# Gate/up, down and per-layer gate products by Strassen's scheme on two problems of 544 tokens

## The chip, the cores and the metric

The kernel runs on one core of one Trainium2 chip. The time is the device time of one execution in microseconds, the median of several runs. The engines have their usual names: PE is TensorE (PEld its weight loads), DVE is VectorE, ACT is ScalarE, POOL is GpSimd, and SP is SyncE, which issues nearly all transfers here.

## The reference

One decoder layer works on 1024 prompt tokens and 64 sample tokens (8 sequences of 8), 1088 rows of 1024 features in all, everything in float32.

```
h  = rmsnorm(x, norm_mix);  q, k, v, ... ga, gb = split(h @ w_in)
o  = select_attend(...);    conv = short_conv(cg * xc, ...)
x += (sigmoid(ga) * o + sigmoid(gb) * (bg * conv)) @ w_out          # 1024 x 1024
h  = rmsnorm(x, norm_ffn);  g, u = split(h @ w_gate_up)             # 1024 x 5632
x += (silu(g) * u) @ w_down                                         # 2816 x 1024
gate = sigmoid(rmsnorm(x, norm_ple) @ w_ple_gate)                   # 1024 x 1024
x += (p @ w_ple) * gate
y  = rmsnorm(x, norm_final)
```

The change concerns the last four matrix products with the 1088 rows: out, gate/up, down and per-layer gate. This part is called the second half here.

## The kernel before

Activations lie transposed in SBUF, features on partitions and the 1088 tokens along the free axis, and each product keeps a weight block of 128 x 128 stationary and moves tokens past it. The tokens go in three chunks, `CH` = 384, 384 and 320. To keep float32 accuracy, every operand is split into a leading part rounded to the fast format (`hi`) and the remainder (`lo`), and each block takes three matmuls: hi·hi, hi·lo and lo·hi. A weight part of at most 512 columns a partition is fetched by SP into `wraw`; ACT writes `wh` from it and POOL subtracts to get `wl`. Two `wraw` and four pairs of `wh`/`wl` are in rotation (class `Weights`).

`run_group` goes chunk by chunk through a block: 24 matmuls into one PSUM bank (tag `pj`, three banks) for a contraction of 1024, and then one evacuation. For gate the evacuation is a Silu on ACT, for up a multiplication on DVE (`silu<-pj,silu`) followed by the split into `m_hi` (ACT) and `m_lo` (POOL). For out and down it is one addition on DVE into the residual `x1` (`x<-pj,x`). Gate/up and down alternate in three groups of 8, 7 and 7 blocks of 128 hidden features, so that `m` stays in SBUF.

Before gate/up and before the per-layer gate stands a norm. Per token chunk, ACT squares (`sq`), DVE adds the squares, PE sums over partitions (`po<-ones,sq`), DVE finds the reciprocal root in some 10 tiny instructions (`ns`), makes a diagonal (`dg`), PE spreads it (`at<-dg,ones`), and DVE, ACT and POOL make `hx`, `h_hi` and `h_lo` for 8 feature blocks. The first and last two blocks of a product are run as pairs per chunk, so that another chunk's products stand in PE's queue while one chunk's norm is worked out.

All engines execute in order. What order they get is decided while the program is built, by the class `Weaver`: it keeps a rough clock of each engine, runs the main stream of products, and lets side streams (norms, softmax, stores) put their instructions in when their inputs should be there. All arithmetic goes through its small helpers, so in the profile line L152 is a projection matmul, L148 another matmul, L159 a transpose, L102 a DVE tensor-tensor operation, L106 a DVE operation with a scalar and two tensors, L111 a DVE scalar operation, L117 a POOL tensor-tensor operation, and L98 an ACT operation.

Of the kernel before, what the change touches and what calls it, by code (L numbers as in the profile page):

```python
# [43 lines left out]


# [5 lines left out]
def tok_tiles(c):  # L51
    c0, n = CH[c]
    return [(c0 // P + j, min(P, T - c0 - j * P)) for j in range(-(-n // P))]

# [17 lines left out]
class Weaver:  # L72
    """Orders the instructions of several streams for the in-order engines."""
# [14 lines left out]
    # instructions, with a rough clock of each engine  # L88
# [29 lines left out]

    def recip(self, out, in_, n):
# [41 lines left out]
    # buffers: the ring of a tag holds the times at which its free ones came free  # L161
# [11 lines left out]
    # streams  # L173
# [104 lines left out]
def hybrid_decoder_step(ctx, tc, I, O):  # L278
# [18 lines left out]
    c2_scr = dram([KT, P, T], F32, "c2_scr")  # L297
    ple_scr = dram([KT, P, T], F32, "ple_scr")
# [4 lines left out]
    pp = ctx.enter_context(tc.tile_pool(name="ps", bufs=1, space=PSUM))  # L303
    PSB = {"pj": 3, "at": 2, "pt": 2, "po": 1}
    for t, n in PSB.items():
        W.add_tag(t, n)

    def psum(tag):
        W.cur.t = max(W.cur.t, W.take(tag))
        return pp.tile([P, 512], F32, tag=tag, name=tag, bufs=PSB[tag])  # L310

# [22 lines left out]
    def new_h(name):  # L334
        H["hi"] = apool.tile([P, KT, T], F32R, tag="A_hi", name=name + "_hi")
        H["lo"] = apool.tile([P, KT, T], F32R, tag="A_lo", name=name + "_lo")
# [15 lines left out]
    def sqrt_table():  # L352
        """Has the table of Sqrt loaded before it is waited for."""
# [5 lines left out]
    # ------------------------------------------------------------------  # L359
    # products with the activations: weight blocks stationary, token chunks moving  # L360
    class Weights:
        """Parts of at most 512 columns a partition: loaded, then split into a leading and a remaining part."""
        NP, NR = 4, 2

        def __init__(self):
            self.parts, self.nl, self.nv = [], 0, 0

        def add(self, src, shape):
            p = dict(src=src, shape=list(shape), done=False)
            self.parts.append(p)  # L370
            return p

        def load(self):
            if self.nl < len(self.parts):
                p = self.parts[self.nl]
                p["raw"] = wpool.tile(p["shape"], F32, tag="wraw", name="wraw", bufs=self.NR)
                p["t"] = W.dma(p["raw"], p["src"])
                self.nl += 1

        def pump(self, must=False, most=9):  # L380
            while most and self.nv < len(self.parts) and (self.nv < self.NP or self.parts[self.nv - self.NP]["done"]):
                p = self.parts[self.nv]
                if not must and p.get("t", 0.0) > W.T["pe"]:
                    break
                must, most = False, most - 1
                if self.nl <= self.nv:
                    W._flush(1e9)
                    while self.nl <= self.nv:
                        self.load()
                old, W.cur = W.cur, Stream(None)  # L390
                W.cur.t = max(W.T["pe"], p["t"])
                p["hi"] = wpool.tile(p["shape"], F32R, tag="wh", name="wh", bufs=self.NP)
                p["lo"] = wpool.tile(p["shape"], F32R, tag="wl", name="wl", bufs=self.NP)
                r = p.pop("raw")
                m = p["shape"][1] * p["shape"][2]
                W.act(p["hi"], r, AF.Copy, m)
# [1560 lines left out]
```

## Time and profile before

| what | value |
|---|---|
| runs | 2037.45, 2044.50 and 2044.59 us, median 2044.5 us |
| profiled execution | span 2039.7 us; it has no time of its own on record beside the span, and the span lies 4.8 us below the median of the runs |
| PE, matmuls | busy 1991.4 us, 98% |
| DVE | busy 918.3 us, 45% |
| ACT | busy 636.1 us, 31% |
| POOL | busy 701.4 us, 34% |
| transfers | 167.88 MB, mean 82 GB/s |

The shares are averages. In the first 1020 us (input projection, attention, convolution) DVE is busy in seven to nine tenths of many slices; in the second half it is busy in none to two tenths for long stretches, while PE shows nine tenths throughout.

### The profile page before, as it was taken

How to read it: one execution, taken by the hardware profiler on the slowest of the kernel's cores; microseconds unless marked ns; L12 is line 12 of the kernel's file. 1: busy time of each engine (PE TensorE's matmuls, PEld its weight loads, DVE VectorE, ACT ScalarE, POOL GpSimd, SP SyncE). 2: the span in 40 equal slices, each digit the busy share in tenths (PEclk: the TensorE clock that was granted, in tenths of full speed). 3: DMA queues.
4: the chain of work that ended last, by engine and by line, in shares of the span. 5: the costliest groups of instructions: out<-in, count | busy, mean ns of one | idle time of the engine just before them, and what ended most of it. 6: DMA issues, size and time to landing. Idle time of an engine off the chain costs nothing.

```text
span 2039.7 us, 31786 instructions
## 1 busy us (share of the span) xinstructions
PE 1991.4 (98%) x12065; PEld 1910.0 (94%) x12065; DVE 918.3 (45%) x2154; ACT 636.1 (31%) x1315; POOL 701.4 (34%) x672
## 2 busy tenths in 40 slices
PE   8999999999999999999999999999999999999998
PEld 5987788999999999779999899999999999999898
DVE  6636999899898885214224400011000110002734
ACT  5355433213433235333422322111222112222333
POOL 2533454223222233114423433322333223332483
PEclk9999999999999999999999999999999999999999
DMA  4664334222222122545541111111111111111133
GB/s 148 189 183 122 95 111 119 64 60 78 66 66 69 51 70 72 141 115 163 191 150 37 42 42 47 47 42 47 47 42 44 41 51 42 47 43 46 43 99 117
DMA packets 252980, 167.88 MB, mean 82 GB/s; under 512 B 26048, under 2 KB 247800, under 8 KB 252826
## 3 DMA queue, kind: packets, MB, share of 16 engines
q1 hardware_dynamic: 252582, 165.74, 27.6%
q8 instruction: 95, 1.56, 0.3%
q14 instruction: 59, 0.48, 0.1%
q10 hardware_dynamic: 244, 0.09, 0.0%
HBM read 126.59 MB, written 39.06 MB: 81 GB/s over the span
## 4 chain that ended last, share of the span: by engine, by line
PE 85%; DVE 5%; issue 1%; ACT 1%; POOL 1%; DMA 0%; SPq 0%; POOLq 0%; DVEq 0%; ACTq 0%
PE pj L152 74%; PE at L148 5%; PE po L148 4%; PE pt L159 3%; DVE hx L106 0%; DVE scores L106 0%; DVE ru L102 0%; DVE h_lo L102 0%; ACT h_hi L98 0%; DVE junk L1050 0%; DVE ns L1618 0%; DVE ns L1620 0%; DVE sq L102 0%; POOL wl L117 0%; POOL psmp L1377 0%
## 5 line engine op out<-in xcount | busy, mean ns | idle before, releaser
L152 PE MATMUL pj<-h_hi,wh 128*128 128x384 f32 (+2 forms) x2616 | 872.1, 333 | 0.3 <-ACT wh L98 0.3
L152 PE MATMUL pj<-h_lo,wh 128*128 128x384 f32 (+2 forms) x2616 | 857.8, 328 | 1.2 <-POOL h_lo L117 1.0
L152 PE MATMUL pj<-h_hi,wl 128*128 128x384 f32 (+2 forms) x2616 | 858.0, 328 | 0.7 <-POOL wl L117 0.7
L117 POOL TENSOR_TENSOR wl<-wraw,wh 128x512 fp32r<-128x512 f32 (+2 forms) x286 | 367.2, 1286 | 760.5 <-ACT wh L98 739.6
L152 PEld LDWEIGHTS pj<-h_hi,wh 128*128 128x128 f32 (+1 forms) x2616 | 493.0, 188 | 16.7 <-issue 12.5
L152 PEld LDWEIGHTS pj<-h_lo,wh 128*128 128x128 f32 (+1 forms) x2616 | 493.3, 189 | 5.6 <-POOL h_lo L117 2.1
L152 PEld LDWEIGHTS pj<-h_hi,wl 128*128 128x128 f32 (+1 forms) x2616 | 492.6, 188 | 1.7 <-POOL wl L117 1.1
L98 ACT ACTIVATE wh<-wraw 128x512 fp32r<-128x512 f32 (+2 forms) x286 | 177.1, 620 | 334.4 <-PE pj L152 310.9
L102 DVE TENSOR_TENSOR silu<-pj,silu 128x384 f32<-128x384 f32 (+1 forms) x66 | 35.3, 536 | 470.4 <-PE pj L152 466.1
L152 PE MATMUL pj<-m_hi,wh 128*128 128x384 f32 (+1 forms) x720 | 235.6, 327 | 0.0
L152 PE MATMUL pj<-m_hi,wl 128*128 128x384 f32 (+1 forms) x720 | 235.1, 327 | 0.0
L152 PE MATMUL pj<-m_lo,wh 128*128 128x384 f32 (+1 forms) x720 | 234.9, 326 | 0.0
L102 DVE TENSOR_TENSOR x<-pj,x 128x384 f32<-128x384 f32 (+1 forms) x96 | 51.4, 535 | 241.8 <-PE pj L152 237.7
L152 PEld LDWEIGHTS pj<-m_hi,wh 128*128 128x128 f32 x720 | 135.2, 188 | 0.3
L152 PEld LDWEIGHTS pj<-m_lo,wh 128*128 128x128 f32 x720 | 135.2, 188 | 0.3
L152 PEld LDWEIGHTS pj<-m_hi,wl 128*128 128x128 f32 x720 | 135.2, 188 | 0.0
L117 POOL TENSOR_TENSOR m_lo<-silu,m_hi 128x384 fp32r<-128x384 f32 (+1 forms) x66 | 64.1, 972 | 157.4 <-ACT m_hi L98 157.4
L1050 DVE TENSOR_SCALAR_CACHE_REDUCE junk<-scores,canda 128x384 uint8<-128x384 f32 (+3 forms) x132 | 107.3, 813 | 4.7
L117 POOL TENSOR_TENSOR rt<-rt,ru 128x384 fp32r<-128x384 f32 (+5 forms) x81 | 81.1, 1008 | 74.5 <-ACT ru L98 33.9
L98 ACT ACTIVATE m_hi<-silu 128x384 fp32r<-128x384 f32 (+1 forms) x66 | 33.5, 507 | 201.8 <-DVE silu L102 201.8
L1131 POOL TENSOR_SCALAR p<-p,mx 128x128 f32<-128x128 f32 (+7 forms) x64 | 50.5, 794 | 100.3 <-DVE mx L121 81.2
L1050 DVE TENSOR_SCALAR_CACHE_REDUCE junk<-scores,candb 128x896 uint8<-128x896 f32 x66 | 80.0, 1213 | 2.3
(244 smaller groups left out, 2149.3 us busy)
## 6 DMA issues: line engine op xcount, KB each, us to landing
wraw<-in_w_in SPq DMA_DIRECT2D x112, 256.0 KB
wraw<-in_w_gate_up SPq DMA_DIRECT2D x88, 256.0 KB
wraw<-in_w_down SPq DMA_DIRECT2D x32, 256.0 KB
x<-in_x_prompt SPq DMA_DIRECT2D x13, 512.0 KB
x<-x_scr SPq DMA_DIRECT2D x8, 544.0 KB
x_scr<-xT SPq DMA_DIRECT2D x8, 512.0 KB
ql<-ql_scr SPq DMA_DIRECT2D x32, 128.0 KB
qh<-qh_scr SPq DMA_DIRECT2D x32, 128.0 KB
```

What stands on the lines that cost most here:

```text
L98: self.nc.scalar.activation(out, in_, func, **kw)
L102: self.nc.vector.tensor_tensor(out, a, b, op=op)
L117: self.nc.gpsimd.tensor_tensor(out, a, b, op=op)
L148: self.nc.tensor.matmul(ps, l, r, start=start, stop=stop)
L152: self.nc.tensor.matmul(ps, l, r, start=start, stop=stop)
L159: self.nc.tensor.transpose(ps, in_, ident)
L1050: nc.vector.tensor_scalar(junk[:m, :L], score[q], cand[:m, i:i + 1].bitcast(F32), None, op0=op, op1=OP.add, accum_out=cnt[:m, i:i + 1])
L1131: nc.gpsimd.tensor_scalar(p[:, :L], p[:, :L], mx[:, 0:1], 1.0, op0=OP.mult, op1=OP.mult)
```

## The change

The 1088 tokens become two problems of 544, each in halves of 272 (`CW`). For gate/up, down and per-layer gate, a product of a 2x2 block matrix (two halves of the contraction, two blocks of 128 outputs) with a 2x2 block of activations (two halves of the contraction, two halves of 272 tokens) is done with 7 products in place of 8. Each of the 7 needs a sum or difference of weights (`wsum`, on DVE) and one of activations (`factors`, on DVE), all split again into `hi` and `lo` (`wh`/`wl`, `f_hi`/`f_lo`); the 7 results are added up as they leave PSUM (`take`). The hidden activations `m` go to memory (`m_scr`) and come back, two 128-feature blocks at a time. Down runs after all of gate/up, in four groups of 3, 3, 3 and 2 pairs of blocks. The out projection stays an ordinary product, first for problem 0, then for problem 1. After the out projection's pools are opened there are 5 banks `pj`, 2 `at` and 1 `po`, and 7 pairs of `wh`/`wl` and 5 `wraw`. In the first half the instructions are the same; their order moves in places, since weight loads are no longer started ahead of the planner's clock.

```diff
+ORDER = (1, 6, 7, 5, 2, 4, 3)
...
+            elif kind == 6:
+                q["s1"], q["s2"] = self.sums(q["items"][3])[:, :n], self.sums(it)[:, :n]
+                W.tt(q["s1"], flat(r21["tile"]), flat(r22["tile"]), OP.add, n)
+                W.tt(q["s2"], q["s1"], flat(r11["tile"]), OP.subtract, n)
...
+            elif kind == 7:
+                src = self.sums(it)[:, :n]
+                W.tt(src, flat(r11["tile"]), flat(r21["tile"]), OP.subtract, n)
...
+            elif kind == 3:
+                src = self.sums(it)[:, :n]
+                W.tt(src, flat(r12["tile"]), q["s2"], OP.subtract, n)
...
+            W.act(flat(h), src, AF.Copy, n)
+
+            def low():
+                (W.tt if kind in (6, 5, 4) else W.pool_tt)(flat(l), src, flat(h).bitcast(F32), OP.subtract, n)
...
+    def factors(p, b, qa, qb, qt, done):
...
+        W.tt(t1, b12, b11, OP.subtract, CW)
+        W.tt(t2, b22, t1, OP.subtract, CW)
+        W.tt(b12, b22, b12, OP.subtract, CW)
+        tb, ta, tt = lead(qb, 2, 2), lead(qa, 0, 2), lead(qt, 4, 2)
...
+        rest(qb, 2, 2, tb, False)
+        W.tt(b21, b21, t2, OP.subtract, CW)
+        tc_ = lead(b21, 6, 1)
...
+        rest(qa, 0, 2, ta, True)
...
+        rest(qt, 4, 2, tt, False)
...
+        rest(b21, 6, 1, tc_, True)
...
+    def take(self, p, i, ps):          # GateUp
+        c11, u, c21, c22, v = self.q1[:, :CW], self.q1[:, CW:], self.q2[:, :CW], self.q2[:, CW:], ps[:, :CW]
+        if i == 1:
+            W.act(c11, v, AF.Copy, CW)
+        elif i == 6:
+            W.tt(u, v, c11, OP.add, CW)
+        elif i == 7:
+            W.tt(c21, v, u, OP.add, CW)
+        elif i == 5:
+            W.tt(c22, v, c21, OP.add, CW)
+            W.tt(u, v, u, OP.add, CW)
...
+    def down_factors(p):
...
+                yield ev_gu[p] if a < 4 else ev_gr[[h for h in range(len(GR)) if any(x[0] == a - 4 for x in pairs_of(h))][0]][p]
...
+    def take(self, p, i, ps):          # Down
...
+            for x in {1: [x11], 6: [au], 7: [x22, x21], 5: [x22, x12], 2: [x11], 4: [x21], 3: [x12]}[i]:
+                W.tt(x, v, x, OP.add, CW)
...
+            if i == 6:
+                for x in (x22, x21, x12):
+                    W.tt(x, x, au, OP.add, CW)
...
-    for f0, nf in ((0, 8), (8, 7), (15, 7)):
-        for f in range(f0, f0 + nf):
-            a = block(I["w_gate_up"], f * P, evac_gate, h_acts, need={"S2": 1}, pre=pre_ev(ev_h2))
-            b = block(I["w_gate_up"], DFF + f * P, evac_up(f - f0), h_acts)
...
+    g_out = out_pass(0) + out_pass(1)
+    g_rest = passes(gu_pair, (0, 1), False) + passes(gu_pair, range(2, NF), True)
+    for gr in range(len(GR) - 1):
+        g_rest += passes(down_pair(gr), range(4), True)
+    g_rest += passes(down_pair(len(GR) - 1), (0, 1), True) + passes(down_pair(len(GR) - 1), (2, 3), False)
+    g_rest += passes(pg_pair, (0, 1), False) + passes(pg_pair, (2, 3), True)
...
+    def run_pair(x, p, last):
+        items, blocks, sink, evs, ev_done = x
+        yield evs[p]
+        tot = 3 * len(blocks)
+        for q_, i in enumerate(ORDER):
...
+            for kk, b in enumerate(blocks):
+                th, tl = factor(p, i, b)
+                for w_, a_ in ((it["hi"], th), (it["hi"], tl), (it["lo"], th)):
+                    W.mmg(ps[:, :CW], w_[:, kk, :], a_, CW, c == 0, c == tot - 1)
```

The following three places show how instructions move. The first is on DVE, in the steady part of gate/up; before, at the end of the out projection and the first two gate/up blocks, DVE has:

```order
L102 TENSOR_TENSOR x_11840<-pj,x_11840 128x320
L102 TENSOR_TENSOR x_11840<-pj,x_11840 128x384 x2
L102 TENSOR_TENSOR x_11840<-pj,x_11840 128x320
L102 TENSOR_TENSOR silu<-pj,silu 128x384 x2
L102 TENSOR_TENSOR silu<-pj,silu 128x320
```

Of the change, most of the second of a gate/up pair's two passes (`q` are places for results; `wsum` and `wl` belong to the next pair's weights):

```order
L121 TENSOR_TENSOR wsum<-wraw 128x512
L121 TENSOR_TENSOR wsum<-wsum,wraw 128x512
L121 TENSOR_TENSOR q_11861<-pj,q_lo 128x272
L121 TENSOR_TENSOR wsum<-wraw 128x512
L121 TENSOR_TENSOR q_11861<-pj,q_11861 128x272
L121 TENSOR_TENSOR q_lo<-pj,q_lo 128x272
L121 TENSOR_TENSOR wl<-wsum,wh 128x512
L121 TENSOR_TENSOR q_lo<-pj,q_lo 128x272
L121 TENSOR_TENSOR wl<-wsum,wh 128x512
L121 TENSOR_TENSOR q_11861<-pj,q_11861 128x272
L121 TENSOR_TENSOR wl<-wraw,wh 128x512
```

Before, DVE had three instructions per gate/up block of 128 hidden features; now it has 7 results and one product per pass, and in every second pass 4 sums of weights and 3 remainders besides.

The second place is on PE, where down ends and the per-layer gate begins. Before, the last down products (on `m`), the sums of squares of the second chunk, and the first per-layer gate products of the first chunk (on `h`):

```order
L152 MATMUL pj<-m_hi,wl 128x320
L152 MATMUL pj<-m_hi,wh 128x320
L152 MATMUL pj<-m_lo,wh 128x320
L152 MATMUL pj<-m_hi,wl 128x320
L148 MATMUL po<-ones,sq 128x1 x3
L152 MATMUL pj<-h_hi,wh 128x384
L152 MATMUL pj<-h_lo,wh 128x384
L152 MATMUL pj<-h_hi,wl 128x384
```

Of the change, the last product of down (`f_hi`, `f_lo` are factors), the norm's instructions of both problems, and the first of the per-layer gate:

```order
L140 MATMUL pj<-f_lo,wh 128x272
L140 MATMUL pj<-f_hi,wl 128x272
L172 MATMUL po<-ones,q_hi 128x1 x3
L172 MATMUL po<-ones,q_hi 96x1
L172 MATMUL po<-ones,q_hi 64x1
L172 MATMUL at<-q_hi,ones 128x272 x2
L172 MATMUL at<-q_lo,ones 128x272 x2
L140 MATMUL pj<-f_hi,wh 128x272
```

Before, 24 products of the first chunk stood behind these sums of squares, ahead of the third chunk's; now no product stands between the end of down and the spreading of both problems' norms.

The third place is on DVE at the same point. Before, between the last step of one chunk's reciprocal root and its `hx`, there is:

```order
L1622 SCALAR_TENSOR_TENSOR ns<-ns 128x3
L111 TENSOR_SCALAR dg<-ident,ns 128x128 x3
L102 TENSOR_TENSOR sq<-sq 128x384
L106 SCALAR_TENSOR_TENSOR hx<-at,gvec,x_11840 128x384 x4
L102 TENSOR_TENSOR h_lo<-hx,h_hi 128x384
```

Of the change, the start of problem 0's normed values and factors:

```order
L125 SCALAR_TENSOR_TENSOR q_hi<-at,gvec,x_11849 128x272 x4
L125 SCALAR_TENSOR_TENSOR q_lo<-at,gvec,x_11849 128x272 x6
L125 SCALAR_TENSOR_TENSOR q_11860<-at,gvec,x_11849 128x272 x2
L121 TENSOR_TENSOR q_11861<-q_hi 128x272
L121 TENSOR_TENSOR q_11861<-q_hi,q_11861 128x272
L121 TENSOR_TENSOR q_hi<-q_hi 128x272
L121 TENSOR_TENSOR q_lo<-q_lo 128x272 x3
L121 TENSOR_TENSOR q_hi<-q_lo 128x272
L121 TENSOR_TENSOR q_hi<-q_11860,q_hi 128x272
L121 TENSOR_TENSOR q_lo<-q_11860,q_lo 128x272
L121 TENSOR_TENSOR f_lo<-q_hi,f_hi 128x544
L121 TENSOR_TENSOR q_hi<-q_hi,q_11861 128x272
```

Where a chunk's feature block took one DVE instruction and every third remainder, a pair of feature blocks now takes four for the normed values, four differences and two remainders of 544 columns.

## Rows read from the trace of the kernel before

**Rows 1.** Windows: us, busy (count) of PE, PEld, DVE, ACT, POOL; clock; DMA, GB/s

```profile
1020.70:1139.40 118.70, 113.24 (x670) 111.16 (x669) 49.22 (x113) 33.54 (x63) 38.06 (x32) 0.99 0.25 83
1139.40:1899.30 759.90, 759.90 (x4616) 759.74 (x4614) 86.23 (x161) 153.47 (x290) 233.60 (x203) 1.00 0.16 45
1899.30:1934.10 34.80, 30.04 (x165) 27.52 (x165) 29.68 (x75) 14.35 (x27) 17.64 (x16) 0.95 0.14 42
1934.10:2010.00 75.90, 75.90 (x452) 75.74 (x452) 28.57 (x48) 28.56 (x60) 59.56 (x56) 0.98 0.28 85
2010.00:2024.10 14.10, 14.10 (x109) 14.08 (x108) 8.84 (x30) 4.73 (x9) 0.95 (x1) 1.00 0.38 136
2024.10:2039.70 15.60, 7.16 (x51) 6.09 (x49) 7.93 (x26) 5.44 (x10) 0.83 (x1) 0.81 0.50 186
```

**Rows 2.** PE instruction groups from 1020.7 us: xcount | busy us, mean ns

```profile
L152 PE MATMUL pj<-h_hi,wh 128*128 128x384 f32 x832 | 281.9, 339 | 0.0
...
L152 PE MATMUL pj<-m_hi,wh 128*128 128x384 f32 x480 | 161.4, 336 | 0.0
...
L152 PE MATMUL pj<-h_hi,wh 128*128 128x320 f32 x416 | 128.8, 310 | 0.0
...
L152 PE MATMUL pj<-m_hi,wh 128*128 128x320 f32 x240 | 74.1, 309 | 0.0
```

**Rows 3.** PE in order of time (start, us): matmuls of 256 and 320 columns

```profile
519.79 0.28 PE L148 MATMUL po<-pth,v_hi 128*128 128x256 f32 x1
...
520.74 0.28 PE L148 MATMUL po<-pth,v_lo 128*128 128x256 f32 x1
...
1207.22 0.30 PE L152 MATMUL pj<-h_hi,wh 128*128 128x320 f32 x1
...
1209.12 0.31 PE L152 MATMUL pj<-h_lo,wh 128*128 128x320 f32 x1
```

**Rows 4.** DVE instruction groups from 1020.7 us on

```profile
L102 DVE TENSOR_TENSOR x<-pj,x 128x384 f32<-128x384 f32 x64 | 35.7, 557 | 177.1 <-PE pj L152 172.9 <-DMA x<-x_scr 4.2
L102 DVE TENSOR_TENSOR sq<-sq 128x384 f32<-128x384 f32 x42 | 26.1, 622 | 42.7 <-ACT sq L98 42.7
...
L106 DVE SCALAR_TENSOR_TENSOR hx<-at,gvec,x 128x384 f32<-128x384 f32 x32 | 18.5, 607 | 4.5 <-PE at L148 4.5
L102 DVE TENSOR_TENSOR x<-pj,x 128x320 f32<-128x320 f32 x32 | 15.7, 491 | 64.7 <-PE pj L152 64.7
...
L106 DVE SCALAR_TENSOR_TENSOR hx<-at,gvec,x 128x320 f32<-128x320 f32 x16 | 7.8, 542 | 1.5 <-POOL m_lo L117 1.0 <-PE at L148 0.5
...
L102 DVE TENSOR_TENSOR h_lo<-hx,h_hi 128x384 fp32r<-128x384 f32 x8 | 7.2, 902 | 0.4
```

**Rows 5.** DVE in order of time, norm before gate/up

```profile
1113.26 0.54 DVE L102 TENSOR_TENSOR x<-pj,x 128x384 f32<-128x384 f32 x1
1113.75 0.59 DVE L106 SCALAR_TENSOR_TENSOR hx<-at,gvec,x 128x384 f32<-128x384 f32 x1
```

**Rows 6.** In order of time, per-layer gate: DVE, then POOL

```profile
1959.07 1.61 DVE L102 TENSOR_TENSOR sq<-sq 128x384 f32<-128x384 f32 x1 [0.39 <-ACT sq L98]
...
1965.02 0.56 DVE L102 TENSOR_TENSOR sq<-sq 128x384 f32<-128x384 f32 x1 [3.95 <-ACT sq L98]
...
1958.96 1.29 POOL L117 TENSOR_TENSOR wl<-wraw,wh 128x512 fp32r<-128x512 f32 x1
1960.24 1.21 POOL L1734 TENSOR_SCALAR x<-x,gvec 128x384 f32<-128x384 f32 x1
```

**Rows 7.** POOL instruction groups from 1020.7 us on

```profile
L117 POOL TENSOR_TENSOR wl<-wraw,wh 128x512 fp32r<-128x512 f32 x150 | 194.3, 1297 | 422.5 <-ACT wh L98 411.2 <-PE pj L152 10.0
L117 POOL TENSOR_TENSOR m_lo<-silu,m_hi 128x384 fp32r<-128x384 f32 x44 | 44.8, 1018 | 133.8 <-ACT m_hi L98 133.8
```

**Rows 8.** Windows in the norm before gate/up, columns as in rows 1

```profile
1120.00:1125.00 5.00, 1.82 (x13) 1.53 (x11) 4.28 (x10) 1.45 (x3) 3.12 (x3) 1.00 0.35 101
1125.00:1130.00 5.00, 5.00 (x20) 4.67 (x20) 2.08 (x14) 1.77 (x2) 0.00 (x0) 0.66 0.12 34
```

More of the change, by code (lines that the diff above doesn't have):

```diff
@@ L380, in pump @@
-        def pump(self, must=False, most=9):
-            while most and self.nv < len(self.parts) and (self.nv < self.NP or self.parts[self.nv - self.NP]["done"]):
-                p = self.parts[self.nv]
-                if not must and p.get("t", 0.0) > W.T["pe"]:
+            self.items, self.ni = [], 0
+            self.raws, self.nl = [], 0
+            self.slots, self.sp = [dict(pool=wpool, tags=("wh", "wl"), bufs=4, last=None) for _ in range(4)], 0
+            self.places, self.rp = [dict(pool=wpool, tag="wraw", bufs=2, last=None) for _ in range(2)], 0
@@ new lines, in free, with low @@
+        def free(self, *raws):
+            for r in raws:
+                r["free"] = True
+                W.later(self.load)
+        def low(self, upto=None):
+            while self.lows and (upto is not None or self.lows[0][0] <= W.T["pe"]):
+                t, fn, it = self.lows.popleft()
+                old, W.cur = W.cur, Stream(None)
+                W.cur.t = t
+                fn()
+                W.cur = old
+                if it is upto:
+                    break
+        def pump(self, must=False, most=9):
+            self.low()
+            while most and self.ni < len(self.items):
+                s = self.slots[self.sp]
+                if s["last"] is not None and not s["last"]["done"]:
+                    break
+                it = self.items[self.ni]
+                if any("t" not in r for r in it["raws"]):
+                    if not must:
+                        break
+                    W._flush(1e9)
+                    while any("t" not in r for r in it["raws"]):
+                        assert self.load(), "no room for a load"
+                t = max([r["t"] for r in it["raws"]], default=0.0)
+                if not must and t > W.T["pe"]:
@@ L402, in hybrid_decoder_step, with want @@
+        def want(self, it):
+            while "hi" not in it:
+                self.pump(True)
+            if "split" not in it:
+                self.low(it)
     wts = Weights()
@@ new lines, in places, with room, getq @@
+    def places(*aps):
+        for ap in aps:
+            Qs.append(ap)
+            W.ring["Q"].append(W.T["pe"])
+    def room(p):
+        pool, a = (apool, "A") if p == 0 else (N_["bp"], "B")
+        fac[p] = [pool.tile([P, 28, CW], F32, tag=f"{a}_{e}", name=f"f{p}_{e}") for e in ("hi", "lo")]
+        for e in ("hi", "lo"):
+            t = pool.tile([P, 2, PW], F32, tag=f"{a}_{e}x", name=f"q{p}_{e}")
+            places(t[:, 0, :], t[:, 1, :])
+    def getq(n):
+        out = []
+        for _ in range(n):
+            W.take("Q")
+            out.append(Qs.popleft())
+        return out
@@ L1739, in hybrid_decoder_step @@
-    ev_x = [[Ev() for _ in range(KT)] for _ in CH]
+        if p not in fac:
+            room(p)
+        yield {"at": 2, "Q": 1}
+        (dg,), bc = getq(1), [psum("at"), psum("at")]
+        for j, (o, m) in enumerate(TT[p]):
+            W.ts(dg[:, o:o + m], ident[:, :m], ns[:, 8 + j:9 + j], None, OP.mult, None, m)
+        yield None
+        for h in range(2):
+            W.mm(bc[h][:, :CW], ones, dg[:, h * CW:(h + 1) * CW], CW, True, True, f32=True)
+        giveq(dg)
+        left, t0 = [4], W.cur.t
@@ new lines, in passes, with gu_pair, down_pair @@
+    def passes(make, js, both):
+        if both:
+            return [(x, (0, 1)) for j in js for x in [make(j)]]
+        return [(make(j), (p,)) for p in range(2) for j in js]
+    def gu_pair(f):
+        return pair_of(I["w_gate_up"], 0, 4, f * P, DFF + f * P), range(4), GateUp(f), ev_h2, ev_gu if f == NF - 1 else None
+    def down_pair(g):
+        f0, n = GR[g]
+        return lambda j: (pair_of(I["w_down"], f0 * P, n, 2 * j * P, (2 * j + 1) * P), [a % 4 for a, _, _ in pairs_of(g)], Down(g, j),
+                          ev_df[g], ev_gr[g] if j == KT // 2 - 1 else None)
@@ L1897, in main @@
         open_late()
[L1898 to L1899 removed]
+        yield from second_half()
     W.spawn(phase_a())
```

643 lines of the change are left out of this document (424 added, 219 removed).

## The prediction

> **What bounds the kernel now.** I first read the windows by stage. From the first out product at 1020.7 us to the last per-layer gate product at 2024.1 us, 1003.4 us pass, and PE is busy through all of it but two stretches: 113.24 of 118.7 us up to 1139.4, and 30.04 of 34.8 us around 1920 [rows 1]. These are the two norms, where products lack their input. In the 759.9 us between, PE runs without a gap at a clock of 1.00 while DVE is busy for 86.2 us and POOL for 233.6 us. So the second half is bounded by PE, and every other engine has room. Over the whole second half DVE is busy 202 us (49.22 + 86.23 + 29.68 + 28.57 + 8.84, the windows before the tail).
>
> The groups of PE give the number of matmuls: 832 + 480 + 416 + 240 = 1968 of one kind, and each block has three kinds, so 5904 [rows 2]. In the steady window 4616 take 759.9 us, .1646 us each, so all take 972 us, and 31 us of the 1003.4 are something else: the two holes, small matmuls, and the clock at restarts.
>
> Behind a hole PE is also slow: in the 5 us after the gap at 1120 it is busy throughout but starts 20 matmuls at a mean granted clock of .66 [rows 8], where .1646 us each would make 30. That costs some 1.7 us.
>
> **Fewer products, shorter ones.** After, the out projection takes 8 blocks x 24 x 2 halves x 2 problems = 768 matmuls, gate/up 22 pairs x 2 problems x 7 x 4 x 3 = 3696, down 11 x 4 x 2 x 7 x 3 = 1848, per-layer gate 4 x 2 x 7 x 12 = 672: together 6984, each of 272 columns. They are more in number, because a matmul now moves 272 columns and not 363 on average. What one costs I take from starts in order of time: 8 steps of 256 columns take .95 us, .1188 each, and 13 steps of 320 columns 1.90 us, .1462 each [rows 3]. On the line between them 272 columns take .1256 us. 6984 x .1256 = **877 us, 95 us less** than 972. (By the 256 and 320 rows alone the sum would lie between 830 and 1021 us; the mean of before, .1646 at 362.7 columns, lies on the same line, so I hold .1256 to 1%, 9 us.)
>
> **What DVE gets.** Its prices come from the groups of DVE. An addition out of PSUM took 557 ns for 384 columns and 491 for 320, 1.05 ns a column, and the next instruction starts some .05 to .07 us before the recorded end [rows 4, 5]. This gives .37 us for 272 columns, .62 for 512 and .655 for 544, .49 for 384, .35 for 256. A normed value out of `at` took 607 and 542 ns, so .42 for 272 columns. A tiny `ns` step is taken as .2. Counting DVE's instructions of the second half in the new order at these prices gives some 690 us, more than three times before.
>
> One price is uncertain. 692 of these instructions read two operands in SBUF, and the trace shows such ones at quite different lengths: `sq` of 384 columns is 622 ns in the mean, 65 ns more than the addition out of PSUM, and `h_lo` 902 ns, 345 ns more [rows 4]. One `sq` took 1.61 us, from 1959.07, ending with the POOL instruction that began at 1958.96 and into the next; another took .56 us with POOL idle [rows 6]. So POOL's work can hold them up. I take +.15 us each, between the two means, and 0 and +.345 as bounds: DVE then has 790 us (690 to 930). The Trainium skill, page SBUF — State Buffer, section "SBUF: two separate sides", says that a DVE operation with two SBUF inputs and a GpSimd operation exclude each other for a whole instruction. The row of 1.61 us agrees; the 42 `sq` with a mean of 622 ns show that it seldom bites in the old order. What the rule would do if it bit each time is the third rival.
>
> In the steady passes this work fits. A gate/up pass on PE is 84 matmuls, 10.55 us. The second of a pair's passes, the heavier, has on DVE seven results, a product, four weight sums and three remainders: 7.6 us, 8.8 with +.15, 10.3 with +.345. A pair of down passes has 10.8 to 13.2 us of DVE against 15.8 of PE. So PE should stay the bound there. POOL has four remainders of 512 columns at 1.3 us [rows 7] and two of 272 per two passes, some 7 of 21 us.
>
> **What waits.** With three times the work, DVE no longer gets through the norms and factors before PE runs out. At each place the new order gives the list of DVE's instructions that must come first, and what PE has in its queue meanwhile. Each line is DVE's time less PE's, with the bounds of +0 and +.345:
>
> - Normed values and factors of problem 1 for gate/up, behind two pairs of problem 0. After the last result of those pairs DVE has 9 instructions of 544 columns, 13 of 272, 8 normed values and 2 of 512: 15.3 us (18.9 with +.15, 23.6 with +.345), and PE has nothing. With a microsecond for rounding on ACT **20 us** (16 to 25).
> - From gate/up to down. Down's factors of the last pairs come from `m` that has only just been made, for both problems: 40.7 us (32.3 to 51.6) against 10.55 + 7.9 us of PE, **22** (14 to 33).
> - Two borders between groups of down, where the next group's factors can only take the places of the last one's: 34.9 us (28.9 to 42.6) against 23.7, with the same microsecond 12 each, **24** (12 to 40).
> - The last group of down, of two pairs of blocks. A pass has 42 matmuls, but still ten results, three additions, the weights, and the squares for the norm. Eight passes: 74.4 us of DVE (62.6 to 89.8) against 8 x 42 x .1256 = 42.2 of PE, **32** (20 to 48).
> - The norm before the per-layer gate, problem 0. PE's queue has no product between down and the spreading of the norms (second piece of order), where 24 products of another chunk stood before. DVE has 8.6 us from the last result to the diagonals (28 tiny steps, four additions of 544), and then 24 normed values, 15 differences of 272, 7 remainders of 544 and five diagonals, 21.2 us, up to the first product's last factor: 33.7 with +.15 (29.8 to 38.8), **34** (30 to 39).
> - The per-layer gate of problem 0, where DVE also makes what is left of the factors: 23.4 us against 21.1, **2** (0 to 7).
> - Normed values and factors of problem 1 for that gate, behind the last result of problem 0: 13.2 us and 2 on ACT, **15** (12 to 18).
>
> Sum: **149 us** (104 to 210). Two items are not of DVE. PE's own sums, spreadings and transposes cost 8 us here (part of the 31 of before), and after each of some nine waits PE restarts at the lower of its two levels, as in rows 8: nine times 1.7 us, part of it within waits already counted, so 10 (5 to 15). Together 167 us in place of the 31.
>
> **What I cost at nothing.** *Transfers.* Out reads its weights for each problem anew, 512 KB per block in 48 x .1256 = 6.0 us, 87 GB/s, and `m` goes out and back, 24.5 MB over 460 us; the trace moved 186 GB/s in the tail [rows 1]. If that cover failed, out would stretch to at most the 118.7 us that it and the norm take now, from 96, +22. *First half.* The instructions are the same, and PE is bound there too, but for some 29 us. Weight loads come a little later; 0, and 8 either way. *Tail.* 15.6 us [rows 1] stay, though the last result and the stores of `y` are now two problems' and not three chunks'; 3 either way.
>
> **The sum.** 1020.7 + 877 + 167 + 15.6 = 2080 us of span. The span of before lies 4.8 us under the median of the runs, so **2085 us**. Break-even is at 31 + 95 = 126 us of waits and PE's extra, that is, some 108 us of waits.
>
> **Rivals.**
>
> *Faster.* The lists above are put wholly behind the last result, as if DVE began each with no start. If DVE works parts of them off while PE still has products, as its queue allows where a list stands among results that come early, the waits shrink toward what the two norms cost before. With PE's other time as before: 1020.7 + 877 + 31 + 15.6 + 4.8 = 1949 us; with half of the 136 us more that I forecast, 2017. It decides as soon as waits fall under 108 us. For it speaks that DVE has some 10 of every 21 us free in gate/up (7.6 us in a second pass, 3.2 in a first), against it that the order puts the factors of a group behind results of the last. Chance .17.
>
> *No change.* POOL and DVE don't hold each other up: waits and restarts at their lower bounds, 104 + 8 + 5 = 117, in place of 167: 2035, and up to 2054 if one or two places keep the forecast's wait. Chance .13.
>
> *Slower still.* Every remainder on POOL holds up a two-input operation. In a second pass of gate/up DVE's 5.0 us of results and product, 5.2 us behind four POOL remainders and 2.6 us of its own then make 12.8 us against 10.55, 2.3 us lost in each of 20 pairs, 45 us, and the time is 2128; with the waits' upper bounds it is over 2150. The row of 1.61 us [rows 6] speaks for it, the mean of 622 ns against. This is what the skill's rule named above would make. Chance .12.
>
> **How the numbers follow.** The forecast, 2085 us, has a chance of .58, with its own range of 2054 to 2125. The measurement tells some 0.5%, 10 us. Faster than 2034: .17 for the first rival and .03 for the low end of the second; within: the second's other .10 and .04 of the forecast; the rest, .66, is slower. To hold 8 in 10, the range takes in the upper half of the first rival and the lower half of the third: 2005 to 2140.
>
> **What the profile after would show.** Matmuls of 272 columns starting every .125 us in gate/up, without gaps; PE busy some 890 us of a second half of some 1040. DVE busy 700 to 900 us there. Holes on PE of 15 to 30 us before the first gate/up of problem 1, at the start of down, at the two borders and twice around the start of the per-layer gate, each ended by a factor (`f_lo`, from DVE, or `f_hi`), with the clock down after them; and PE at about 55 to 60% in the last group of down, waiting for PSUM banks that DVE empties. The chain of waits should run over DVE at these places. I am wrong if the holes come to less than 108 us, if gate/up's passes take more than 10.7 us, or if DVE's two-input operations take under .7 us for 544 columns throughout.

## The result and the profile after

The changed kernel takes 2190.4 us (median of 4 runs, 2189.9 to 2193.9) against 2044.6 us of before: a ratio of 1.072, with a 95% interval of 1.0695 to 1.0745. It is slower by 146 us. The forecast was slower by 41 us (2085, range 2005 to 2140): the sign held, the size did not, and the time lies above the range.

The profiled execution has a span of 2188.2 us. The windows of the changed kernel by stage (columns as in [rows 1]) are: out projection; the first two gate/up pairs of both problems; the rest of gate/up; the first three groups of down; the last group and the norm; the per-layer gate; the tail.

```profile
1030.50:1140.90 110.40, 102.43 (x782) 100.81 (x783) 57.87 (x106) 38.26 (x67) 54.10 (x42) 0.97 0.42 128
1140.90:1214.10 73.20, 51.51 (x352) 48.50 (x351) 67.75 (x119) 28.50 (x52) 32.33 (x24) 0.81 0.21 62
1214.10:1636.10 422.00, 422.00 (x3362) 422.00 (x3361) 271.01 (x468) 123.23 (x225) 123.83 (x82) 1.00 0.26 81
1636.10:1900.30 264.20, 215.17 (x1514) 206.91 (x1513) 227.43 (x437) 86.22 (x173) 103.69 (x87) 0.88 0.26 76
1900.30:2030.90 130.60, 68.44 (x366) 59.29 (x364) 106.30 (x261) 37.87 (x85) 31.98 (x34) 0.70 0.11 33
2030.90:2165.50 134.60, 100.19 (x700) 96.76 (x700) 107.68 (x161) 50.74 (x92) 81.60 (x56) 0.87 0.22 68
2165.50:2188.20 22.70, 13.13 (x94) 10.93 (x92) 12.72 (x30) 9.63 (x15) 0.00 (x0) 0.87 0.54 197
```

The third row is the scheme as it was meant: 3360 products in 422.0 us, .1256 us each, PE without a gap at a clock of 1.00, with DVE busy 64% of it. This is to the digit the interval that the prediction drew between two rows [rows 3]. The rows around it show the price. In the last group of down and the norm behind it (fifth row) PE is busy for half of the time, at a mean granted clock of .70, while DVE is busy for 106 of 131 us; in [rows 1] PE was busy for 30.04 of the 34.8 us around that norm, and without a gap before them.

From here on, what a stretch loses is its length less its products times .1256 us. The 6984 products take 877.2 us.

| stretch | forecast | measured |
|---|---|---|
| start of the second half, later by | 0 (8 either way) | 9.8 |
| out projection | 0 | 13.9 |
| norm before gate/up, first two pairs | 20 | 31.0 |
| rest of gate/up | 0 | 0.0 |
| down: start and two borders | 22 + 24 | 74.3 |
| last group of down, norm before the gate | 32 + 34 | 88.4 |
| per-layer gate | 2 + 15 | 50.2 |
| PE's own work and restarts, not assigned to a place | 18 | (within the rows above) |
| tail, longer by | 0 (3 either way) | 7.1 |
| sum | 167 | 274.7 |

167 and 274.7 differ by the 108 us that the span misses the forecast by (2188.2 against 2080). Of these, 95 lie where DVE's work was reckoned against PE's (11 at the norm before gate/up, 28 in down, 22 in the last group and the norm, 33 in the gate), less the 18 that had no place, and 31 lie in the start, out and the tail.

### The profile page after: what moved, and what is told of

It is laid out like the page before. It is cut to its first block, busy times and chain, and to the rows that moved or that the text cites. A ratio compares the mean times of both kernels' runs of the same rounds, so it can differ in the third digit from the quotient of the medians.

```text
span 2188.2 us, 36488 instructions
## 1 busy us (share of the span) xinstructions
PE 1967.5 (90%) x13177; PEld 1863.9 (85%) x13177; DVE 1552.9 (71%) x3277; ACT 769.9 (35%) x1561; POOL 785.9 (36%) x687
## 3 DMA queue, kind: packets, MB, share of 16 engines
q1 hardware_dynamic: 284502, 199.70, 31.1%
## 4 chain that ended last, share of the span: by engine, by line
PE 72%; DVE 15%; issue 5%; DMA 3%; POOL 2%; ACT 1%; SPq 1%; DVEq 0%; POOLq 0%; ACTq 0%
PE pj L140 34%; PE pj L176 27%; PE at L172 5%; PE po L172 4%; PE pt L183 3%; DVE f_lo L121 2%; DVE q_lo L121 2%; DVE q_hi L121 2%; DVE x L121 1%; DVE q L121 1%; DVE wsum L121 1%; POOL wl L136 1%; SPq L149 1%; DVE wl L121 1%; DMA wraw<-in_w_in 1%
## 5 line engine op out<-in xcount | busy, mean ns | idle before, releaser
L140 PE MATMUL pj<-f_hi,wh 128*128 128x272 f32 x2072 | 618.3, 298 | 64.5 <-ACT f_hi L117 38.1
L140 PE MATMUL pj<-f_hi,wl 128*128 128x272 f32 x2072 | 617.4, 298 | 39.0 <-POOL wl L136 21.0
L140 PE MATMUL pj<-f_lo,wh 128*128 128x272 f32 x2072 | 616.0, 297 | 33.6 <-POOL f_lo L136 27.6
L136 POOL TENSOR_TENSOR wl<-wraw,wh 128x512 fp32r<-128x512 f32 (+3 forms) x246 | 328.9, 1340 | 663.8 <-ACT wh L117 627.8
L140 PEld LDWEIGHTS pj<-f_hi,wh 128*128 128x128 f32 x2072 | 406.7, 196 | 72.6 <-ACT f_hi L117 41.5
L140 PEld LDWEIGHTS pj<-f_hi,wl 128*128 128x128 f32 x2072 | 406.6, 196 | 45.4 <-DVE wl L121 22.8
L140 PEld LDWEIGHTS pj<-f_lo,wh 128*128 128x128 f32 x2072 | 405.8, 196 | 40.4 <-POOL f_lo L136 32.4
L176 PE MATMUL pj<-h_hi,wh 128*128 128x384 f32 (+2 forms) x1197 | 406.2, 339 | 0.3 <-ACT wh L117 0.3
L176 PE MATMUL pj<-h_hi,wl 128*128 128x384 f32 (+2 forms) x1197 | 393.6, 329 | 0.7 <-POOL wl L136 0.7
L176 PE MATMUL pj<-h_lo,wh 128*128 128x384 f32 (+2 forms) x1197 | 393.1, 328 | 0.0
```

The source lines that it names most:

```text
L136: self.nc.gpsimd.tensor_tensor(out, a, b, op=op)
L140: self.nc.tensor.matmul(ps, l, r, start=start, stop=stop)
L176: self.nc.tensor.matmul(ps, l, r, start=start, stop=stop)
```

## The experiments

Two theories were set against each other. **Theory A**: PE waits for DVE's work, which is too much ahead of a product, and dearer beside POOL. **Theory B**: the amount would fit, but the planner reckons DVE's instructions too cheap and so puts instructions into PE's and DVE's queues where they block what could run.

The runs were taken in several rounds, in which the kernel before took 2041.3 to 2046.2 us. For differences of a few us the ratio to it, given in brackets with its 95% interval, is therefore safer than the microseconds.

**The scheme undone stage by stage.** The same two problems, staging and traffic, but 8 products for 8 in a stage. The edit gives a pair of blocks its four weights unsummed, leaves the factors without differences, and takes each result out of PSUM once:

```diff
+    def plain_factors(p, b, qa, qb, done):
...
+        if plain:
+            return [[wts.add(part(r, c), [P, nk, P]) for r in (rows, rows + nk * P)] for c in plain(c1, c2)]
...
+    def run_plain(x, p, last):
+        for o, its in enumerate(items):
+            for h in range(2):
...
+                for half, it in enumerate(its):
+                    for kk, b in enumerate(blocks):
+                        for w_, a_ in ((it["hi"], th), (it["hi"], tl), (it["lo"], th)):
+                            W.mmg(ps[:, :CW], w_[:, kk, :], a_, CW, c == 0, c == tot - 1)
+                sink.plain_take(p, o, h, ps[:, :CW])
```

Gate undone, expected: 

> The per-layer gate as an ordinary product on the same two problems (8 products for 8: 96 matmuls of 272 columns more, 12 us of PE; no sums of weights, 4 of 7 factors per pair of feature blocks). Theory A (PE waits for the DVE work listed ahead of a product): the wait at the norm before the gate falls by some 15 us and the 50 us lost in the gate itself to some 20; with 12 us more of PE the time is about 2157 us. Theory B (the order of PE's queue costs it: the spreading of problem 1's norm stands ahead of problem 0's first product): the hole of 20 us at that spreading stays, time 2180 us or more.

Measured: 2140.5 us (ratio 1.048, 1.044 to 1.052), 50 us less than the change, more than theory A asked (33) and far from theory B. The loss falls in both of the stretches concerned: in the last group and the norm from 88.4 to 63.7 us, in the gate from 50.4 to 15.9.

Gate and down undone, expected: 

> Down ordinary too (264 matmuls more, 33 us of PE; a result takes one addition on DVE and not 10 for 7 products; no weight sums). Theory A: the 30 us lost at the start of down, the 45 us at two borders of groups and some 40 us in the last group fall to 25 together, 57 us net gain: about 2100 us. Theory B (order of the queues and the clock, not the amount of DVE work): the losses stay, about 2190 us.

Measured: 2058.9 us (1.008, 1.006 to 1.011), another 82 us less, where theory A had asked for 57. The windows of this run for down's first three groups, the last group with the norm, and the gate:

```profile
1636.80:1869.60 232.80, 222.54 (x1730) 221.65 (x1729) 57.90 (x117) 47.64 (x87) 77.69 (x69) 0.98 0.28 87
1869.60:1930.70 61.10, 52.86 (x410) 52.10 (x408) 38.41 (x84) 27.70 (x50) 27.93 (x30) 0.94 0.27 79
1930.70:2037.10 106.40, 106.03 (x833) 105.36 (x833) 56.46 (x90) 41.48 (x82) 64.47 (x47) 0.98 0.30 96
```

Down has 216 products more here (1728), and is done 31 us sooner: DVE is busy for 57.9 us in place of 227.4, and the loss falls from 74.3 to 15.8 us. In the second row 48 more products take less than half of the change's time (61.1 us, after 105.9 with the gate alone undone and 130.6 in the change), with the clock at .94 in place of .70.

All undone, expected: 

> Gate/up ordinary as well: two problems of 544, the same staging through memory, no Strassen anywhere. 528 matmuls more in gate/up, 66 us of PE; the 31 us lost at the norm before gate/up fall to some 15. Theory A: about 2150 us, so gate/up by the scheme alone is worth some 50 us. If even gate/up's scheme is worth nothing, the time is that of the run with gate and down ordinary, or lower.

Measured: 2090.6 us (1.024, 1.021 to 1.026), 32 us slower than with gate/up by the scheme; theory A had put that gain at some 50. So gate/up is the one stage where the scheme pays: 66 us of products saved, 28 of them lost at its norm (31.1 us against 2.8) and 7 in down's first groups (15.8 against 8.5). Undone in this order, the scheme saves 33 us in down and costs 115, and saves 12 in the gate and costs 62; the last group's loss belongs to both.

**POOL taken away from DVE.**

```diff
+                if self.sums is not None and kind not in (6, 5, 4):
+                    W.go("pool", 0.12 + n * 0.00225)
+                    it["lo"] = h
```

and the same for the factors' remainders on POOL; the products read the leading part in their place, so the results of this kernel are not those of the reference. Expected: 

> All of the change, but POOL's remainders of weights and factors in the second half are left out (the products read the leading part in their place); DVE, ACT and PE have the same instructions in the same order. Theory A with POOL as the cause of the price (DVE operations with two operands in SBUF took .43, .68, .72 us for 272, 512, 544 columns with POOL idle, and .90, 1.03, 1.05 on the average beside POOL): such operations take the shorter time throughout, DVE has some 160 us less, and the waits fall by some 65 us and restarts by 10: about 2115 us. Theory B (order): a fall of 20 us at most, 2170 us or more.

Measured: 2120.4 us (1.038, 1.035 to 1.042), 70 us less than the change. The groups of DVE in the second half, first of the changed kernel:

```profile
L121 DVE TENSOR_TENSOR x<-pj,x 128x272 f32<-128x272 f32 x288 | 116.9, 433 | 81.9 <-PE pj L140 70.3 <-DMA x<-x_scr 3.7 <-ACT q_lo L117 3.6
L121 DVE TENSOR_TENSOR wl<-wsum,wh 128x512 fp32r<-128x512 f32 x60 | 60.3, 1006 | 2.1 <-ACT wh L117 2.1
L121 DVE TENSOR_TENSOR wsum<-wraw 128x512 f32<-128x512 f32 x60 | 50.4, 840 | 0.0
L121 DVE TENSOR_TENSOR f_lo<-q_hi,f_hi 128x544 fp32r<-128x544 f32 x43 | 37.8, 882 | 0.0
```

and of the run without POOL's remainders:

```profile
L121 DVE TENSOR_TENSOR x<-pj,x 128x272 f32<-128x272 f32 x288 | 118.0, 435 | 98.7 <-PE pj L140 89.9 <-ACT q_lo L117 3.6 <-ACT q L117 2.1
L121 DVE TENSOR_TENSOR wsum<-wraw 128x512 f32<-128x512 f32 x60 | 42.7, 712 | 0.0
L121 DVE TENSOR_TENSOR wl<-wsum,wh 128x512 fp32r<-128x512 f32 x60 | 41.3, 689 | 2.4 <-ACT wh L117 2.4
L121 DVE TENSOR_TENSOR f_lo<-q_hi,f_hi 128x544 fp32r<-128x544 f32 x43 | 30.6, 716 | 0.0
```

What comes out of PSUM takes the same time in both (433 and 435 ns). The weights' remainders fall from 1006 to 689 ns, the factors' from 882 to 716. From the first out product to the last one of the gate DVE is busy 838 us with POOL and 704.5 without, 133.5 us for the 692 operations with two operands in SBUF, .19 us each. The losses of the stretches fall from 257.8 to 190.3 us. But 190.3 us remain, with hardly a collision left (POOL is busy for 34.6 us there, 32.8 of them in the gate).

The run takes away two things at once: what POOL costs DVE, and PE's waits for POOL's own remainders. In the change 50 of the 175 us that PE stood between the first and the last product ended with a `wl` or `f_lo` from POOL. How much of the 67.5 us either is worth this run doesn't tell. That the last to arrive is not always what costs the time shows in the next run, where such waits come to 24 us and the losses are no smaller (263 us).

**Order.** Only the planner's price of such operations is raised, by .235 us:

```diff
-        self.go("dve", 0.1 + n * 0.00104)
+        self.go("dve", 0.1 + n * 0.00104 + (0.0 if ps else self.two))
```

Expected: 

> The change with one number of the planner altered: in the second half its price of a DVE operation with two operands in SBUF is raised by .235 us, the mean that the trace of the change showed; instructions are the same, their order is planned anew. Theory A (the amount of DVE work ahead of the products): no place gets less to wait for, 2180 to 2200 us. Theory B (the planner placed instructions too early, and they block the queues): 30 us or more come back, 2160 us or less.

Measured: 2195.3 us (1.073, 1.070 to 1.076, the change's 1.072), no gain, as theory A has it. The new order does move losses: the gate loses 38.6 us in place of 50.4, down and the last group 14 more. Then the one place that looks most like a blocked queue. PE in order of time in the changed kernel, between the spreading of problem 0's norm, that of problem 1's, and the first product of the gate:

```profile
1997.10 2.18 PE L172 MATMUL at<-q_hi,ones 128*128 128x272 f32 x4 [1.77 <-DVE q_hi L130]
2019.26 2.18 PE L172 MATMUL at<-q_lo,ones 128*128 128x272 f32 x4 [19.98 <-DVE q_lo L130]
2030.90 0.59 PE L140 MATMUL pj<-f_hi,wh 128*128 128x272 f32 x1 [9.47 <-ACT wh L117]
```

```diff
+        if p == 1 and ev is ev_h3[1]:
+            yield ev_h3[0]
```

Expected: 

> The change, but the norm of problem 1 before the per-layer gate begins only when problem 0's factors are through, so that its spreading stands behind problem 0's first products in PE's queue and its diagonals behind problem 0's factors in DVE's. Theory B (order): the two holes of 20 and 10 us around that spreading shrink to some 15 together, 2172 us or less. Theory A (amount): problem 0's first product still waits for most of the same list, and what is put off is waited for at problem 1's: 2183 us or more.

Measured: 2182.5 us (1.0665, 1.0637 to 1.0692), 8 us less than the change, or 11 by the ratios: just under the 2183 that theory A set, and far from theory B's 2172. With problem 1's spreading out of the way, the first product follows the first spreading directly, and waits nearly as long:

```profile
1999.54 2.18 PE L172 MATMUL at<-q_hi,ones 128*128 128x272 f32 x4 [1.77 <-DVE q_hi L130]
2024.37 0.59 PE L140 MATMUL pj<-f_hi,wh 128*128 128x272 f32 x1 [22.65 <-ACT wh L117]
```

33.8 us from one to the other before, 24.8 now. It is DVE's list of normed values and factors that lasts: DVE is busy for 32.6 of the 33.9 us from 1997.0 to 2030.9. In the two orders tried, order is worth some 10 us of the 146 at most, and theory B falls as the main cause; that no order could do better is not shown.

**What the scheme is worth in gate/up alone.** From here on gate and down are ordinary. Out's first weights were late: in the change PE stands for 5.78 us up to 1050.17 for weights that ACT had not got, since 4.4 MB of x were asked for ahead of them. The edit fetches them first, and x block by block:

```diff
-        for p, n in ((0, 1), (1, 4)):
-            for k in range(0, KT, n):
-                W.dma(x1[:, k:k + n, p * PW:(p + 1) * PW], x_scr[:, k:k + n, p * PW:(p + 1) * PW])
...
+        for i, (_, p, k, b) in enumerate(g_out):
+            for nx in {0: [2, 3], 1: [4, 5], 2: [6, 7]}.get(i, [i + 5] if i + 5 < 16 else []):
+                x_load(nx // KT, nx % KT)
```

Expected: 

> Scheme in gate/up alone (as in the run with gate and down ordinary, 2059 us), and the first weights of the out projection are fetched ahead of x, and x feature block by feature block, a few blocks ahead of its use, in place of 4.4 MB at once. If the 11 us lost in the first half of out are SP's queue and the transfers, 8 to 10 come back: 2050 us. If not (weights' rounding or PSUM), 2059 us.

Measured: 2049.7 us (1.0017, 1.0007 to 1.0028), and the window of out's first half is 48.60 us with PE at 48.59, where the change had 59.3 us. With the planner's price raised besides, expected: 

> The same with the planner's price of two-operand DVE work raised as above. Theory A: within 5 us of the run beside it. Theory B: the 31 us at the norm before gate/up fall to 20 or less, 10 us faster or more.

Measured: 2051.3 us (1.0026, 1.0010 to 1.0041), no gain: the 31 us at the norm before gate/up stay.

**Cover for the norm before the gate.** All four pairs of the last group problem by problem (`range(4), False` in place of `(0, 1), True` and `(2, 3), False`). Expected: 

> As the run with the scheme in gate/up alone and out's loads reordered (2050 us), but in the last group of down all four pairs go problem by problem, so that 24 us of problem 1's products and not 12 stand behind problem 0's last result while its norm is worked out (two pairs of weights are fetched and split twice for it). Theory A: of the 12.8 us lost there some 9 come back, 2041 us. If the two extra pairs' POOL work or fetches matter, 2050 us or more.

Measured: 2046.8 us (1.002, 1.0005 to 1.0035). The 3 us under 2049.7 are no gain, since the kernel before was faster by 4 in this round: the ratio is the one of the run without the edit (1.0017), and the 2041 missed. The loss there falls from 12.8 to 2.1 us, and 9.7 us turn up one stretch later, in the gate's first pairs (3.4 to 13.1): a wait moved, not removed.

**Less DVE work at the norm before gate/up.** Problem 0's first pairs as ordinary products; the one factor that they need and the scheme doesn't is kept in four places of results.

```diff
+    g_rest = [(gu_early(j), (0,)) for j in range(2)] + [(gu_pair(j), (1,)) for j in range(2)] + ...
```

Two pairs, expected: 

> The same, and the first two gate/up pairs of problem 0 are ordinary products, 24 matmuls (6 us of PE with both) more: they need neither sums of weights nor differences of factors, so DVE has some 20 us less ahead of problem 1's normed values and factors. Theory A: the 31 us lost at the norm before gate/up fall to some 10, net gain 15 us: 2026 us, faster than the kernel before. If what is waited for there is not DVE's work, 6 us slower than the run beside it.

Measured: 2062.0 us (1.008, 1.006 to 1.010). Three pairs, expected: 

> The same with three such pairs in place of two: 36 more matmuls of problem 0 stand over problem 1's norm, 3 of the 12 us more per pair being the scheme's gain forgone and problem 1 taking its weights apart. Theory A: if two pairs cover all, 3 us slower than with two; if problem 1's list is still longer than the cover, up to 8 us faster.

Measured: 2055.4 us (1.005, 1.003 to 1.007). Neither brought the gain; only the step from two pairs to three, 7 us faster, came as its expectation allowed. The reason that fits the trace, which no run isolates, is one of their own: with the four places gone, problem 0's normed values had no place until problem 1's tiles opened. DVE in the run with two pairs made the diagonals during out, and the first normed values 49 us later:

```profile
1088.16 2.00 DVE L131 TENSOR_SCALAR q<-ident,ns 128x128 f32<-128x128 f32 x5
...
1136.92 1.72 DVE L126 SCALAR_TENSOR_TENSOR q<-at,gvec,x 128x272 f32<-128x272 f32 x4
```

So out lost 31.0 us, where it had lost 3.2. The pairs behind it lost little: with three pairs their 540 products took this window of 69.8 us, 67.8 of them products, a loss of 2 us where 31 had been. This fits theory A without showing it, since DVE could also work in the 28 us that out lost more.

```profile
1161.60:1231.40 69.80, 69.80 (x542) 69.68 (x541) 62.75 (x97) 31.66 (x61) 39.02 (x29) 0.97 0.28 85
```

**A version of about the time of before.** Down in smaller groups, so that the next group's factors have places of their own, and weight loads of the first half started ahead again:

```diff
-    GR = [(0, 3), (6, 3), (12, 3), (18, 2)]
+    GR = [(0, 1), (2, 2), (6, 2), (10, 2), (14, 2), (18, 2)]
...
-                    if not must:
+                    if not must and self.sums is not None:
```

Expected: 

> Scheme in gate/up alone, out's loads reordered (2050 us), and two more edits: down's contraction in groups of 1, 2, 2, 2, 2 and 2 pairs in place of 3, 3, 3 and 2, so that the factors of the next group have places of their own and are there before the border; and in the first half weight loads may again be started ahead of the planner's clock. Theory A: the 16 us lost at down's start and borders fall to 5 or less, for 16 us more of DVE additions that have cover: 2039 us; if the 10 us by which the second half began later were the loads, 2030 us. Otherwise 2039 to 2041, or 2050 if the borders' loss is not the factors' places.

Measured: 2036.4 us (median of 10 runs) against 2042.8 of before: ratio .9964, .9947 to .9980, a difference clear of noise but only .4%. Its windows for down's first five groups, and the last with the norm:

```profile
1628.20:1850.30 222.10, 219.79 (x1730) 219.29 (x1730) 90.38 (x181) 55.86 (x121) 86.34 (x101) 0.99 0.31 95
1850.30:1911.40 61.10, 52.85 (x410) 52.09 (x408) 37.89 (x83) 26.71 (x48) 27.00 (x29) 0.95 0.27 79
```

Down's 1728 products take 222.1 us in place of 232.8; 5 us are lost, as theory A had it. The first half got nothing back: out's first product starts at 1033.0 us, against 1030.5 in the change and 1020.7 of before (1028.9 to 1034.1 over all runs with two problems). Where those 10 us come from stays open; the order of the first half differs from before in many places even so.

## Why the prediction was right in direction and wrong in size

**The products.** Right: 6984 of .1256 us. So the saving of 95 us was there in full.

**Where it waits.** Right in place: every hole that the prediction listed is in the trace, and gate/up's steady passes were no bound. The stages undone show that the scheme's work ahead of products is the cause, as the prediction had it. Two things differ. In the last group PE stood for weights (21 us of its waits there ended with `wh` or `wl`) and hardly for PSUM banks that DVE empties (.7 us). And POOL, which the prediction counted as no bound, ended the longest hole of the gate:

```profile
2084.75 0.60 PE L140 MATMUL pj<-f_hi,wl 128*128 128x272 f32 x1 [20.16 <-POOL wl L136]
```

This `wl` stood in POOL's queue behind residual additions and the factors' remainders, while DVE worked on the same factors until 2082.4 us. In the run without POOL's remainders this place has holes of 8.1, 1.7 and 5.5 us, so POOL made it longer and is not the whole of it.

**The price beside POOL.** The term was +.15 us for an operation with two operands in SBUF; it measured .19 in the sum of DVE's time, so DVE had 838 us (forecast 790, bounds 690 to 930). Without POOL the waits fell by 67.5 us, PE's waits for POOL itself among them, where the forecast and its lower bound lay 45 us apart. This is at most some 22 us of the 108. With POOL idle these operations cost what an addition out of PSUM costs, and the difference between `sq` and `h_lo` that the prediction saw in [rows 4] was POOL: in the kernel before, the 28 of the 42 `sq` with POOL idle took 558 ns in the mean, and the two such `h_lo` 543. The Trainium skill, page SBUF — State Buffer, section "SBUF: two separate sides", gives the cause: such an operation and one of GpSimd that reads SBUF lock each other out of a shared pair of ports. The trace agrees, with 1006 against 689 ns for two operands in SBUF, and 433 against 435 for one in PSUM. The third rival, built on its hitting each time in gate/up, did not come: that stage lost 0.0 us. (Its 2128 is some 2130 by its own terms, which changes nothing.)

**The step that failed: a wait as DVE's time less PE's.** The prediction took each place as two lists that run side by side, so that the longer sets the time. In the last group and the norm, DVE was busy 106.3 us, and the prediction had given it 74.4 + 33.7 = 108.1. Its work was right there. But the stretch took 130.6 us: for 24 us DVE stood as well, 21 of them in the last group, which took 89.2 us with DVE busy for 68.4. Collisions are not the cause: in the run without POOL's remainders DVE stands for 24 us too (columns as in [rows 1]).

```profile
1858.50:1978.80 120.30, 67.44 (x367) 59.41 (x365) 96.07 (x260) 37.32 (x83) 0.00 (x0) 0.70 0.13 37
```

The changed kernel in order of time, in the middle of the last group (all engines, without most of the matmuls):

```profile
1965.99 0.43 PE L140 MATMUL pj<-f_hi,wl 128*128 128x272 f32 x1
1966.45 0.44 DVE L121 TENSOR_TENSOR x<-pj,x 128x272 f32<-128x272 f32 x1 [1.37 <-PE pj L140]
1966.81 0.71 DVE L121 TENSOR_TENSOR q_lo<-q_lo,q 128x544 f32<-128x544 f32 x1
1967.56 0.72 DVE L121 TENSOR_TENSOR q_lo<-q_lo,q_hi 128x544 f32<-128x544 f32 x1
1968.20 0.42 DVE L121 TENSOR_TENSOR wsum<-wraw,wsum 128x256 f32<-128x256 f32 x1
...
1968.72 0.42 ACT L117 ACTIVATE wh<-wsum 128x256 fp32r<-128x256 f32 x1 [7.78 <-DVE wsum L121]
...
1969.19 0.60 PE L140 MATMUL pj<-f_hi,wh 128*128 128x272 f32 x1 [2.77 <-ACT wh L117]
...
1971.31 0.44 DVE L121 TENSOR_TENSOR x<-pj,x 128x272 f32<-128x272 f32 x1 [2.69 <-PE pj L140]
...
1972.21 0.43 PE L140 MATMUL pj<-f_hi,wl 128*128 128x272 f32 x1
```

PE has no weights and stands for 2.77 us. They come from a sum that stands in DVE's queue behind two additions of squares and behind a result of PE's last product. When the sum is made, ACT rounds it and PE starts; now DVE's next instruction is a result of the product that PE has just begun, and DVE stands for 2.69 us. The two engines take turns. 13.7 us of DVE's idle time in this stretch ended with a product for `x`; from 1940 to 1990 us DVE alone is busy for 15 us, PE alone for 18, and both for 15. A subtraction of sums can't see this. The same form of loss fits the per-layer gate, with 50 us for a forecast of 17 at 107.7 us of DVE in 134.6, and down's groups, with 74 for 46. There it was read from busy times only (of DVE's idle time 16 us in the gate and 26 in down ended with PE) and not followed turn by turn, so how much of their excess it makes stays open.

**The clock.** The prediction gave 10 us to restarts. Of the 6984 products 326 start .20 to .26 us after the one before, in place of .1256, at the lower of the two levels: .1 us each, 33 us. In the rows above the twelve matmuls from 1969.19 to 1972.21 us take 3.0 us where eleven steps of .1256 make 1.4. PE had stood for 2.77 us before them, and the granted clock is .50 from 1965.0 to 1972.6 us and .60 from 1960 to 1980; so this turn of PE's took twice as long. Part of this hides behind DVE, so the 33 us are no sum to be added.

**Costed at nothing.** Out lost 13.9 us, 10.7 of which came back when the first weights were fetched ahead of x. The prediction held the rate of the transfers against that of the tail [rows 1], and did not ask what stands ahead of the first weights in SP's queue; its upper bound of 22 us holds it. The start of the second half came 9.8 us later, just outside 8, and the tail took 7.1 us more, outside 3.

**The rivals.** That DVE's backlog clears behind PE is true for the steady part of gate/up alone. That POOL and DVE don't collide is refuted by the run without POOL's remainders, and even that run, at 2120 us, lies far above the 2035 that the rival gave, since the waits without collisions are 190 us and not 117.

## What to carry to other kernels

Saving an eighth of the products is a trade of PE's time for DVE's, and here it paid only in the stage whose steady part is long against its start: in gate/up (22 pairs on one set of factors) it paid 32 us of 66, in down and the gate, where factors are made anew for every 4 pairs of outputs, it cost some 3 and 5 times what it saved. When two engines feed each other through in-order queues, don't take the longer of two sums for the time: look for a result of the one that stands ahead of the next input of the other, and add the turns, with the products at the interval that the trace shows behind a hole (.20 to .26 us here). An experiment that undoes the change stage by stage gives such a balance in three runs.

## What was not expected of the hardware

The holding up by POOL reaches tiny operations of DVE too. In the run with the scheme in gate/up alone and out's loads reordered, steps of the reciprocal root on 128 x 5 elements took .15 to .17 us and, beside POOL, 1.27, each in the chain that the norm waits for:

```profile
1144.72 1.56 POOL L137 TENSOR_TENSOR wl<-wraw,wh 128x512 fp32r<-128x512 f32 x1 [0.85 <-ACT wh L118]
1145.04 1.27 DVE L1860 SCALAR_TENSOR_TENSOR ns<-ns 128x5 f32<-128x5 f32 x1
1146.23 0.43 DVE L122 TENSOR_TENSOR q<-pj,q 128x272 f32<-128x272 f32 x1
1146.58 0.15 DVE L1856 TENSOR_TENSOR ns<-ns 128x5 f32<-128x5 f32 x1
```

It ends as the POOL instruction of 512 columns does, which began .3 us before it. So what this one cost came from the POOL instruction that it met, and not from its own size. Another such step, .61 us beside the end of the POOL instruction before, fits; most had POOL idle.
